# A weights ring 32 bytes lower: the addresses of two operands of TensorE, on a decoder trunk

## The chip, the core and the metric

The kernel runs on one core of a Trainium2 chip. The metric is the device time of one execution in microseconds; the figure for a kernel is the median of its runs. SBUF, the working memory, has 128 partitions; a tile of n float32 columns takes 4n bytes in each, from the same address on. Here "address" always means that byte address within a partition, and "remainder" the address modulo 256.

## The reference, cut to what matters

Two layers of a decoder trunk on x of 512 tokens by 1024 features, all in float32:

```
h  = RMSNorm(x);  p = h @ W_in                      # columns for four mixers and their gates
x += W_o( sum over mixers m of sigmoid(gate_m) * (mixer_m(p) @ P_m) )   # MLA, HGRN2, S5, RWKV-7
x += CrossAttn(RMSNorm(x), RMSNorm(mem))            # 4 heads, 256 memory tokens
x += ConvGLU-FFN(RMSNorm(x))                        # width 2816
```

and a last RMSNorm. Most of the arithmetic is products of an activation matrix with a weight matrix of 1024, 512 or 2816 rows.

## The kernel before

Activations are kept transposed, a tile of 128 features by 512 tokens at a time. Every weight matrix is cut into blocks of 128 x 128, and the host lays all blocks down in the order in which they are used (w_order). `Ring` streams them: eight blocks are a chunk, one DMA fills `raw` (three buffers of 4 KB per partition), ScalarE rounds it into `whi` (line 238) and VectorE makes the rest, `wlo` (line 239; two buffers of each). MLA and the gated unit of S5 have small rings of their own. An activation is split the same way: hh and hl (for the projection, the output, the queries and the feed-forward's first products), oh and ol (mixers' outputs in the merge), ah and al (the feed-forward's last product), mh and ml (memory).

A dense product is then three matmuls per block, into one PSUM bank (`dense`, lines 331 to 333):

```
nc.tensor.matmul(ps[:, :N], hi, xh, start=i == 0, stop=False)
nc.tensor.matmul(ps[:, :N], hi, xl, start=False, stop=False)
nc.tensor.matmul(ps[:, :N], lo, xh, start=False, stop=i == n - 1)
```

The first operand is the stationary one, 128 columns that TensorE loads ahead (LDWEIGHTS in the profile, "PEld"); the second is the moving one, 512 columns (256 for the memory's keys). While a matmul streams its moving operand from one address, the next one's weights are loaded from another. In `dense_t` (lines 353 to 355) the activation is the stationary operand and the ring the moving one.

A layer goes: projection with the four mixers (MLA, HGRN2, S5, RWKV-7) woven into it, their small F32 matmuls between the dense ones; merge with the gates (lines 569 to 587); keys and values of the memory, output projection, cross attention; feed-forward. The order is that of the program, found by a scheduler with priorities; it plays no part in the change.

Where a tile lies is decided by pools. On the left of SBUF they follow each other upwards: `const`, `hp` (hh and hl), `sm` (small statistics), the ring, and then the pools of a stage (memory, x, RWKV-7, MLA, keys and values of the cross attention). On the right other pools grow downwards: HGRN2, S5, merge (oh, ol), queries and probabilities of the cross attention, feed-forward (ah, al). Four tiles named pad0 to pad3 are never read or written; they only take room. In the built program of before, hh, hl, the ring, mh, ml, x, oh, ol, ah, al, q, pT and the keys and values all start at remainder 128; MLA's ring and activations at 160; S5's ring and activations at 128. hh starts at 28288, whi at 74112, wlo at 82304.

The functions that the diff touches follow; lines are those of the profile.

Of the kernel before, what the change touches and what calls it, by code (L numbers as in the profile page):

```python
# [9 lines left out]
F32 = mybir.dt.float32  # L10
# [12 lines left out]
P = 128  # L23
# [189 lines left out]
class Ring:  # L213


    def __init__(self, T, name, pool, raw_bufs, bufs):
        self.T, self.name, self.pool, self.rb, self.b = T, name, pool, raw_bufs, bufs
        self.n = CHUNK[name]
        self.order, self.dram, self.pos = ORDERS[name], T.A[name], 0
        self.raws = {}  # L220
# [32 lines left out]
class Trunk:  # L253
    def __init__(self, ctx, tc, A):
        self.tc, self.nc, self.A, self.ctx = tc, tc.nc, A, ctx
        nc = self.nc
        self.const = self.pool(ctx, "const")
        self.const.tile([P, 48], F32, name="pad0")
        self.hp = self.pool(ctx, "hp")
        self.sm = self.pool(ctx, "sm")  # L260
        self.sm.tile([P, 56], F32, name="pad1")
        self.pool(ctx, "pr", side="right").tile([P, 24], F32, name="pad2")
        self.ps = self.pool(ctx, "ps", space=PSUM)
        self.ring = Ring(self, "w", self.pool(ctx, "ring"), 3, 2)
        self.vec = self.const.tile([P, L, NVEC], F32, name="vec")
        nc.sync.dma_start(out=self.vec, in_=A["vec"])
        self.halves = self.const.tile([P, L, 24], F32, name="halves")
        o = VOFF["w0"]
        nc.vector.tensor_scalar(out=self.halves, in0=self.vec[:, :, o:o + 24], scalar1=0.5, scalar2=None, op0=ALU.mult)
        self.ident = self.const.tile([P, P], F32, name="ident")  # L270
        self.ones = self.const.tile([P, 1], F32, name="ones")
        nc.vector.memset(self.ones, 1.0)
        dp = self.pool(ctx, "dram", space=bass.MemoryType.DRAM)
        self.r_d = [dp.tile([3, 4, P, S], F32, name=f"r_d{l}") for l in range(L)]
        self.xk_d = [dp.tile([KD, P, MEM], F32, name=f"xk_d{l}") for l in range(L)]
        self.c_d = dp.tile([3, P, S], F32, name="c_d")
        self.su_d = dp.tile([4, P, 4, P], F32, name="su_d")
        self.sy_d = dp.tile([4, P, 4, P], F32, name="sy_d")
        self.x_d = dp.tile([KD, P, S], F32, name="x_d")
        self.o_d = [dp.tile([4, P, S], F32, name=f"o_d{m}") for m in range(4)]  # L280
        self.g_d = dp.tile([4, 8, P, S], F32, name="g_d")
# [1356 lines left out]
```

## Time and profile before

| | us |
|---|---|
| median of 3 runs | 2774.59 |
| lowest and highest | 2773.11, 2781.51 |
| profiled execution, its own time | 2776.61 |
| its span, first to last instruction | 2774.5 |

In that span TensorE is busy for 98%, its weight loads for 80%, VectorE for 65%, ScalarE for 40% and GpSimd for 2%; the 16 DMA engines move 114 GB/s on the mean. Matmuls are pipelined: a record of 0.39 us begins before the one ahead of it has ended, so what a stream of them costs is the step from one start to the next, and it is read from a timeline or from a window that holds nothing else. The granted clock stands in the view by windows as a share of full speed. "Idle before" is the time in which an engine had nothing under way, and what ended it.

### The profile page before, as it was taken

Reading aid. Unit: us, or ns where it says so; the run is one execution under the profiler, and the core shown is the slowest. Engines: PE = TensorE matmul, PEld = TensorE weight load, DVE = VectorE, ACT = ScalarE, POOL = GpSimd, SP = SyncE. Lnnn points to the kernel's source line nnn. Section 1 sums busy time; section 2 is a strip of 40 time slices with the busy share of each in tenths; the row PEclk is TensorE's granted clock in tenths of the full one; section 3 lists DMA queues with packets and bytes.
Section 4 is the critical chain, followed back from the end, with each engine's and each line's share of the span. In section 5 each row is a group of like instructions: output and inputs, shape, how many; then the busy total and the mean of one; then the engine's idle time right before and its main releaser. Section 6 shows DMA issues by size and latency. Waiting matters only on the chain.

```text
span 2774.5 us, 37768 instructions
## 1 busy us (share of the span) xinstructions
PE 2714.2 (98%) x14176; PEld 2211.9 (80%) x14176; DVE 1816.6 (65%) x3784; ACT 1112.5 (40%) x1766; POOL 46.5 (2%) x155
## 2 busy tenths in 40 slices
PE   7999999999999999999999999999999999999997
PEld 6878877877788888888888878778777888888886
DVE  6678789675576566546466787797655855664563
ACT  5333343345554443223243333443565534432232
POOL 1000000000000000000000000000000000000000
PEclk9999999999999999999999999999999999999999
DMA  6322233233673233333343232333437632233332
GB/s 196 96 74 71 72 104 103 95 126 110 224 247 120 84 99 97 95 97 99 125 134 99 74 94 63 108 100 98 131 112 254 211 106 77 92 99 98 92 99 76
DMA packets 134534, 315.71 MB, mean 114 GB/s; under 512 B 18384, under 2 KB 38480, under 8 KB 134352
## 3 DMA queue, kind: packets, MB, share of 16 engines
q1 hardware_dynamic: 134352, 313.31, 36.2%
q8 instruction: 112, 1.84, 0.3%
q14 instruction: 70, 0.57, 0.1%
HBM read 266.32 MB, written 45.61 MB: 112 GB/s over the span
## 4 chain that ended last, share of the span: by engine, by line
PE 64%; DVE 5%; DMA 1%; issue 1%; ACT 1%; SPq 0%; DVEq 0%; POOL 0%; ACTq 0%
PE mm L332 17%; PE mm L331 17%; PE mm L333 17%; DVE wlo L239 1%; PE rwy L659 1%; PE hg L1372 1%; PE rw L659 1%; PE mm L354 1%; PE mm L355 1%; PE rw L1520 1%; PE mm L353 1%; PE rw L1016 1%; DVE rdg L924 1%; DVE rdg L926 0%; PE rw L1035 0%
## 5 line engine op out<-in xcount | busy, mean ns | idle before, releaser
L331 PE MATMUL mm<-hh,whi 128*128 128x512 f32 x2144 | 851.2, 397 | 3.1 <-ACT wa L473 2.4
L332 PE MATMUL mm<-hl,whi 128*128 128x512 f32 x2144 | 851.0, 397 | 0.1
L333 PE MATMUL mm<-hh,wlo 128*128 128x512 f32 x2144 | 849.5, 397 | 0.0
L238 ACT ACTIVATE whi<-raw 128x1024 fp32r<-128x1024 f32 (+1 forms) x404 | 418.6, 1037 | 740.5 <-PE mm L332 607.8
L239 DVE TENSOR_TENSOR wlo<-raw,whi 128x1024 fp32r<-128x1024 f32 (+1 forms) x404 | 482.8, 1195 | 294.8 <-ACT whi L238 285.6
L331 PEld LDWEIGHTS mm<-hh,whi 128*128 128x128 f32 x2144 | 404.9, 189 | 88.8 <-ACT wa L473 2.9
L332 PEld LDWEIGHTS mm<-hl,whi 128*128 128x128 f32 x2144 | 405.1, 189 | 85.8 <-issue 4.7
L333 PEld LDWEIGHTS mm<-hh,wlo 128*128 128x128 f32 x2144 | 405.4, 189 | 82.3 <-issue 2.3
L331 PE MATMUL mm<-ah,whi 128*128 128x512 f32 x352 | 136.9, 389 | 0.0
L332 PE MATMUL mm<-al,whi 128*128 128x512 f32 x352 | 136.9, 389 | 0.0
L333 PE MATMUL mm<-ah,wlo 128*128 128x512 f32 x352 | 136.9, 389 | 0.0
L588 DVE TENSOR_TENSOR x<-mm,x 128x512 f32<-128x512 f32 x64 | 44.2, 690 | 123.1 <-PE mm L333 123.1
L331 PE MATMUL mm<-oh,whi 128*128 128x512 f32 x256 | 99.9, 390 | 1.6 <-ACT g L559 1.1
L333 PE MATMUL mm<-oh,wlo 128*128 128x512 f32 x256 | 99.6, 389 | 0.0
L332 PE MATMUL mm<-ol,whi 128*128 128x512 f32 x256 | 99.6, 389 | 0.0
L711 DVE TENSOR_TENSOR gt<-mm,rstd 128x512 f32<-128x512 f32 x44 | 30.5, 692 | 98.2 <-PE mm L333 94.3
L924 DVE TENSOR_TENSOR rdg<-rdg,rE 128x2 f32<-128x2 f32 (+30 forms) x248 | 84.0, 339 | 3.5
L718 ACT ACTIVATE cv<-cv 128x512 f32<-128x512 f32 x44 | 27.8, 632 | 129.7 <-DVE cv L716 129.7
L333 PEld LDWEIGHTS mm<-ah,wlo 128*128 128x128 f32 x352 | 66.1, 188 | 13.7
L331 PEld LDWEIGHTS mm<-ah,whi 128*128 128x128 f32 x352 | 66.1, 188 | 13.7
L332 PEld LDWEIGHTS mm<-al,whi 128*128 128x128 f32 x352 | 66.1, 188 | 13.7
L721 DVE TENSOR_TENSOR up<-mm,rstd 128x512 f32<-128x512 f32 x44 | 30.4, 692 | 63.9 <-PE mm L333 63.9
(511 smaller groups left out, 4158.0 us busy)
## 6 DMA issues: line engine op xcount, KB each, us to landing
raw<-w SPq DMA_DIRECT2D x384, 512.0 KB, 3.6
g_d<-g SPq DMA_DIRECT2D x64, 256.0 KB, 2.1
gin<-g_d SPq DMA_DIRECT2D x64, 256.0 KB, 3.7
oin<-o_d SPq DMA_DIRECT2D x32, 256.0 KB, 3.6
mt<-memT SPq DMA_DIRECT2D x32, 128.0 KB, 3.4
x<-xT SPq DMA_DIRECT2D x16, 256.0 KB, 5.6
raw<-wm SPq DMA_DIRECT2D x12, 256.0 KB, 2.9
xk_d<-xkt SPq DMA_DIRECT2D x16, 128.0 KB, 2.5
```

What stands on the lines that cost most here:

```text
L238: nc.scalar.activation(out=self.hi, in_=raw, func=AF.Copy)
L239: nc.vector.tensor_tensor(out=self.lo, in0=raw, in1=self.hi.bitcast(F32), op=ALU.subtract)
L331: nc.tensor.matmul(ps[:, :N], hi, xh, start=i == 0, stop=False)
L332: nc.tensor.matmul(ps[:, :N], hi, xl, start=False, stop=False)
L333: nc.tensor.matmul(ps[:, :N], lo, xh, start=False, stop=i == n - 1)
L353: nc.tensor.matmul(o, xh[:, ts], wh, start=first, stop=False)
L588: self.nc.vector.tensor_tensor(out=self.x[n], in0=ps, in1=self.x[n], op=ALU.add)
L659: nc.tensor.matmul(out, x, y, start=first and n == 0, stop=last and n == 2)
L711: nc.vector.tensor_tensor(out=gt[:, 2:], in0=ps, in1=rs, op=ALU.mult)
L718: nc.scalar.activation(out=cv, in_=cv, func=AF.Silu)
L721: nc.vector.tensor_tensor(out=up, in0=ps, in1=rs, op=ALU.mult)
L924: V.tensor_tensor(out=tmp[:, :n, :t + 1], in0=M[:, :t + 1, :n].rearrange("p s c -> p c s"), in1=E[:, t, :t + 1].unsqueeze(1).to_broadcast( ...
```

## The change

One pad becomes 32 bytes shorter, 48 float32 columns in place of 56:

```diff
         self.sm = self.pool(ctx, "sm")
-        self.sm.tile([P, 56], F32, name="pad1")
+        self.sm.tile([P, 48], F32, name="pad1")
         self.pool(ctx, "pr", side="right").tile([P, 24], F32, name="pad2")
         self.ps = self.pool(ctx, "ps", space=PSUM)
         self.ring = Ring(self, "w", self.pool(ctx, "ring"), 3, 2)
```

All that is allocated on the left after it starts 32 bytes lower: the small statistics of `sm`, the ring (whi from 74112 to 74080), mh and ml, x, the tiles of RWKV-7, MLA with its ring, and the cross attention's keys and values. `const`, hh and hl lie ahead of it and stay; all on the right stays, with oh, ol, ah, al, q, pT and all of HGRN2 and S5. So ring and hh, hl, ah, al, oh, ol differ by 32 in the remainder instead of 0; ring and mh, ml, and everything within MLA or S5, by 0 as before. The instructions of each engine, their order and their waits are the same in both programs.

## Rows read from the trace of the kernel before

**Rows 1.** Page, part 1: busy time, share of the span and instructions by engine.
```profile
PE 2714.2 (98%) x14176; PEld 2211.9 (80%) x14176; DVE 1816.6 (65%) x3784; ACT 1112.5 (40%) x1766; POOL 46.5 (2%) x155
```

**Rows 2.** View by tile, whi: records in ns (min/median/max), first and last start, shapes.
```profile
L331 PE MATMUL mm<-hh,whi x2144: 387/389/795, 46.4 to 2696.6; 128*128 128x512 f32 x195
...
L238 ACT ACTIVATE whi<-raw x404: 613/1061/1072, 5.3 to 2746.2; 128x1024 fp32r<-128x1024 f32 x126, 128x512 fp32r<-128x512 f32 x9
...
L239 DVE TENSOR_TENSOR wlo<-raw,whi x404: 665/1224/1234, 6.4 to 2747.3; 128x1024 fp32r<-128x1024 f32 x126, 128x512 fp32r<-128x512 f32 x9
...
L331 PE MATMUL mm<-ah,whi x352: 389/389/389, 1148.0 to 2756.4; 128*128 128x512 f32 x176
...
L331 PE MATMUL mm<-oh,whi x256: 389/389/499, 754.2 to 2212.7; 128*128 128x512 f32 x128
```

**Rows 3.** View by windows, tile mm on TensorE: length, busy, count, clock, DMA share.
```profile
1000.00:1388.00 388.00, 386.26 (x1706) 1.00 0.34 102
2370.00:2755.00 385.00, 383.25 (x1690) 1.00 0.30 92
```

**Rows 4.** Timeline of TensorE, 1143 to 1147 us: start, length, line, operation (17 rows).
```profile
1143.24 0.39 PE L331 MATMUL mm<-hh,whi 128*128 128x512 f32 x1
...
1146.86 0.39 PE L332 MATMUL mm<-hl,whi 128*128 128x512 f32 x1
```

**Rows 5.** Timeline of TensorE, 1391 to 1395 us, 256 columns (25 rows).
```profile
1391.78 0.28 PE L331 MATMUL mm<-mh,whi 128*128 128x256 f32 x1
...
1394.66 0.28 PE L331 MATMUL mm<-mh,whi 128*128 128x256 f32 x1
```

**Rows 6.** Timeline of TensorE, 805 to 808 us, layer 0's merge.
```profile
805.29 0.47 PE L331 MATMUL mm<-oh,whi 128*128 128x512 f32 x1 [0.49 <-DVE gin L580]
805.60 0.39 PE L332 MATMUL mm<-ol,whi 128*128 128x512 f32 x1
...
806.75 0.40 PE L331 MATMUL mm<-oh,whi 128*128 128x512 f32 x1
...
807.68 0.39 PE L332 MATMUL mm<-ol,whi 128*128 128x512 f32 x1
```

**Rows 7.** View by lines at 806.76 us: busy, mean ns of one.
```profile
L331 PE MATMUL mm<-oh,whi 128*128 128x512 f32 x1 | 0.4, 397 | 0.0
```

**Rows 8.** Timeline of TensorE, 593 to 595 us: from MLA back to the projection.
```profile
593.12 0.39 PE L332 MATMUL rw<-cql,whi 128*128 128x512 f32 x1
593.35 0.40 PE L333 MATMUL rw<-cqh,wlo 128*128 128x512 f32 x1
...
594.51 0.39 PE L333 MATMUL mm<-hh,wlo 128*128 128x512 f32 x1
```

**Rows 9.** Timeline of the weight loads, near 806.75 and near 1146.86 us.
```profile
806.75 0.19 PEld L332 LDWEIGHTS mm<-ol,whi 128*128 128x128 f32 x1
...
1146.87 0.19 PEld L333 LDWEIGHTS mm<-hh,wlo 128*128 128x128 f32 x1
```

**Rows 10.** By windows, line 332 on TensorE: mixers and merges, both layers.
```profile
90.00:680.00 590.00, 175.84 (x434) 0.99 0.30 94
680.00:940.00 260.00, 135.78 (x349) 1.00 0.57 181
1500.00:2078.00 578.00, 169.00 (x414) 0.99 0.31 95
2078.00:2310.00 232.00, 122.54 (x313) 0.99 0.57 182
```

**Rows 11.** View by lines, shapes apart: out<-moving,stationary; busy us, mean ns.
```profile
L353 PE MATMUL mm<-whi,hh 128*128 128x256 f32 x128 | 38.4, 300 | 0.0
...
L659 PE MATMUL rwy<-pT,xv 128*128 128x512 f32 x96 | 29.5, 412 | 0.0
...
L659 PE MATMUL rw<-xk,q 128*128 128x256 f32 x192 | 28.0, 289 | 0.0
```

**Rows 12.** Page, part 6: DMA issues, KB each, us to landing.
```profile
raw<-w SPq DMA_DIRECT2D x384, 512.0 KB, 3.6
```

## The prediction

> **What bounds the kernel now.** I read the totals by engine first. TensorE is busy for 2714.2 of 2774.5 us and VectorE for 1816.6 [rows 1], so a step pays only through TensorE, and everything added to TensorE's stream counts nearly in full. In the long dense stretches the granted clock is 1.00 [rows 3], its upper level (2.4 GHz), and the change gives it no reason to move.
>
> Then the view by tile of whi: it gives the shortest, median and longest record of each kind of matmul [rows 2]. The 352 records with ah on line 331 all last 389 ns, those with oh and hh have 389 ns as their median. Records overlap, so a record is longer than the step from one start to the next. The step comes from windows and timelines. Two stretches that hold little but the output projection, the queries, the cross attention's output and the feed-forward give 1706 matmuls in 386.26 us and 1690 in 383.25 us [rows 3], 226.4 and 226.8 ns each; I use **226.6 ns**. One piece of the timeline shows it directly: from 1143.24 to 1146.86 us lie 16 steps, 226 ns each [rows 4]. I call that the regular beat.
>
> The beat is not all column time. With 256 columns 24 steps take 2.88 us [rows 5], 120 ns each. The second 256 columns thus cost 106.6 ns, and 120 - 106.6 leaves about **13.4 ns per matmul** that no column explains.
>
> The timeline after a pause is what decides my forecast. At 805.29 us a matmul has waited 0.49 us; from 805.60 to 807.68 nothing waits, yet nine steps take 2.08 us, 231.1 ns each, with records of up to 0.40 us, and only from 807.68 on is it 0.39 and the regular beat [rows 6]. The same instructions on the same tiles run at two paces, and settle in the faster one. In the lines view of that spell one record takes 397 ns [rows 7], 8 more than on the beat. So there is a timing relation between the two reads of TensorE, the moving operand and the next weights, that costs 0 to 8 ns when it is off, and which the present placement lets settle.
>
> One place shows the two reads with different address remainders already. As the built program places them, MLA's weights and activations both start at 160 modulo 256; hh, hl and the main ring at 128. Around 593.35 us the stream changes from one set to the other, so one moving tile is read beside weights 32 bytes away. The record ahead of it is 0.39 and its own 0.40, and five steps from there take 1.16 us, 232 ns each, with no wait named [rows 8]. A single crossing throws the stream off its beat.
>
> **The change part by part.** The pad is one tile; no instruction, wait or DMA is added, removed or reordered on any engine. What moves is the address of everything allocated on the left after it: the rings, the memory tiles mh and ml, x, xk and xv go from 128 to 96 modulo 256. hh, hl, ah, al, oh, ol, q and pT stay.
>
> *Dense matmuls of the main ring.* Each weight block serves three instructions, on lines 331, 332 and 333, as often as one another. With hh and hl that makes 2144 x 3, with ah and al 352 x 3, with oh and ol 256 x 3: 8256 [rows 2]. Those on the beat can lose it; those already off it, behind an interruption, have nothing to lose. The two long stretches hold 1706 + 1690 [rows 3]. The merges with their surroundings hold (349 + 313) x 3 = 1986, with means of 135.78 / 349 = 389 and 122.54 / 313 = 391 ns [rows 10]: close to the beat. The mixers hold (434 + 414) x 3 = 2544 with means of 405 and 408 ns [rows 10], many of them next to a wait or an F32 matmul; with a median of 389 [rows 2] I take half, 1272. Together 1706 + 1690 + 1986 + 1272 = **6654**.
>
> The price of one is not in the trace, since no long stretch has the new difference. From the dear side the 397 ns record gives +8 ns. From the cheap side the whole 13.4 ns could go. Nearest are the two stretches that are off the beat with no wait: 231.1 - 226.6 = 4.5 [rows 6] and 232 - 226.6 = 5.4 [rows 8]. I take **5 ns**: 6654 x 5 = 33.3 us. The weight load starts with the matmul ahead of it to within 0.01 us, on the beat (1146.86 us) and off it (806.75 us) [rows 4, 6, 9], so I see nothing that lets the hardware shift the load by the time of 32 bytes and settle as before.
>
> The Trainium skill, in "TensorE: Matmul & The Clock Gate", section "Step-by-step: what each phase is for", says that TensorE reads moving operand and weights through two independent ports and that loading the next weights takes no read bandwidth from the running matmul. By that rule the sum would be 0 us and not 33. The spells of rows 6 and 8 don't decide against it outright, for they might be a matter of issue; it is the second rival below.
>
> *Smaller products.* In HGRN2's values hh and hl are the weights and the ring the moving operand: 128 x 3 of 256 columns. Queries by keys: 192 of 256. Values by probabilities: 96 of 512 [rows 11]. 672 x 5 ns = 3.4 us; about half stand beside a wait, so 1.7 us.
>
> *What does not change its relation.* Keys and values of the memory (mh, ml and ring move together), MLA (all left) and the gated unit of S5 (all right): 0 us. They are a control inside the kernel.
>
> *VectorE, ScalarE, DMA.* The splits of a chunk take 1061 and 1224 ns by the median [rows 2], while a chunk's 24 matmuls take 24 x 226.6 = 5.4 us; a raw chunk lands after 3.6 us [rows 12] with three buffers. Should the 32 bytes slow any of them by half, they stay hidden; if the landing grew beyond two chunks, 10.9 us, TensorE would wait next.
>
> Sum: 33.3 + 1.7 = **35 us**. The profiled execution took 2776.6 us and would go to 2811.6; it lies 2.0 us above the median of 2774.6 us. From the median: **2810 us**, slower by 1.3%. Likeliest case's own range: 3 to 8 ns, 6654 x 3 = 20 to 6654 x 8 = 53 us, so 2795 to 2830 with the smaller products.
>
> **The rivals.**
>
> *Faster: the fixed 13.4 ns are the price of equal remainders.* If moving operand and weights get in each other's way because they start at the same remainder, 32 bytes would part them. All of it gone: 6654 x 13.4 = 89 us, 2686 us; the case decides from 1.3 ns per matmul on (8.3 us, 0.3%, which is about what a measurement of this kernel can tell from no change). For it: the 13.4 ns are there on the beat in each matmul [rows 4, 5]. Against it: the crossing in MLA, where the difference is 32 already, shows a longer record and not a shorter one [rows 8]. The Trainium skill's page named above gives columns / 2.4 + 2.5 ns as the gap of a warm matmul (section "Back-to-back issue gap"), 216 ns here, which would leave about 11 ns to gain; no stretch read here runs at that. Chance 0.13.
>
> *No change: the addresses don't matter, or the stream settles on an equal beat.* Then the off-beat spells are a matter of issue after a wait, and the crossing in MLA is one of ring or PSUM bank. For it: hh lies an odd and ah an even multiple of 256 bytes from the ring, and both run at 389 ns [rows 2]; the spell with oh has equal remainders throughout [rows 6]. Against it: at the crossing nothing waits. 2775 us. Chance 0.21.
>
> *Dearer: every affected matmul runs at the worst record,* 397 ns, also those that are off the beat now: 8256 x 8 = 66 us and 672 x 8 = 5 us, 2846 us. For it: nothing but that record [rows 7]; a fixed difference could hold the stream at one bad point as well as at a mean. It is the end of the slower case, with 0.08 of its chance.
>
> That the change doesn't do what it says is excluded: in the built program the ring starts 32 bytes lower, and hh, ah and oh stay.
>
> **How the numbers follow.** Slower 0.66 (the forecast with 0.58 and the dearest end with 0.08), no change 0.21, faster 0.13. The range takes in no change with its scatter (2771) and the dearest end (2846); left out are the faster case and a little at both ends, under 2 in 10.
>
> **What would show it.** Right: the records with ah, 389 ns in each of 352 now, go to 392 to 397; the 1706 matmuls of the first long stretch take about 395 us; the 256-column steps with mh stay at 120 ns, since there both operands moved; VectorE, ScalarE and DMA keep their durations. Wrong: ah still at 389 (no change) or well below (faster); or the memory's matmuls slow down as well, which would mean that the distance is not what counts; or more idle time of TensorE behind whi, wlo or raw.

## The result, and the profile after

| | before | after |
|---|---|---|
| median (runs) | 2773.85 us (4) | 2812.98 us (4) |
| lowest and highest | 2772.92, 2781.51 | 2803.09, 2815.53 |
| profiled execution, its own time | 2776.61 | 2813.34 |
| its span | 2774.5 | 2811.1 |

The kernel became slower: the ratio is 1.0126 with an interval of [1.0106, 1.0146], 39 us by the medians and 36.6 us by the two spans. The forecast was 2810 us.

The first line of the page's part 1 answers to [rows 1].

```profile
PE 2756.9 (98%) x14176; PEld 2209.7 (79%) x14176; DVE 1817.7 (65%) x3784; ACT 1113.5 (40%) x1766; POOL 46.5 (2%) x155
```

The same number of instructions on each engine. TensorE's busy time went from 2714.2 to 2756.9 us, 42.7 more; VectorE and ScalarE were busy for 1 us more each, too little for any stage to notice. Span less busy time, the time in which TensorE had nothing under way, went the other way: from 60.3 (2774.5 - 2714.2) to 54.2 us (2811.1 - 2756.9).

The view by tile of whi answers to [rows 2]: records in ns as min/median/max, first and last start.

```profile
L331 PE MATMUL mm<-hh,whi x2144: 387/396/795, 41.7 to 2731.5; 128*128 128x512 f32 x195
...
L331 PE MATMUL mm<-ah,whi x352: 393/395/397, 1161.5 to 2793.1; 128*128 128x512 f32 x176
...
L331 PE MATMUL mm<-oh,whi x256: 392/396/438, 761.3 to 2236.1; 128*128 128x512 f32 x128
...
L331 PE MATMUL mm<-mh,whi x128: 278/283/582, 6.5 to 1433.0; 128*128 128x256 f32 x128
```

Before, every one of the 352 records with ah lasted 389 ns; now the shortest of them lasts 393. The medians of hh and oh went the same way, to 396. The last line is the control inside the kernel: mh moved together with the ring, and its median is 283 ns in both programs. Its line of before is this one.

```profile
L331 PE MATMUL mm<-mh,whi x128: 277/283/582, 6.8 to 1412.4; 128*128 128x256 f32 x128
```

ScalarE's rounding into whi is where it was, at a median of 1060 ns (1061 before).

The view by windows of tile mm on TensorE answers to [rows 3], over nearly the same two stretches of work, which lie 10 to 35 us later.

```profile
1010.00:1405.00 395.00, 393.53 (x1686) 1.00 0.32 99
2400.00:2790.00 390.00, 388.54 (x1664) 1.00 0.29 89
```

393.53 / 1686 = 233.4 ns and 388.54 / 1664 = 233.5 ns a matmul, against 226.4 and 226.8. The clock is 1.00 in both. A piece of the timeline answers to [rows 4]: start and length in us.

```profile
1154.78 0.39 PE L332 MATMUL mm<-hl,whi 128*128 128x512 f32 x1
...
1157.82 0.40 PE L333 MATMUL mm<-hh,wlo 128*128 128x512 f32 x1
```

13 steps in 3.04 us are 233.8 ns each, with no wait, and the records alternate between 0.39 and 0.40. The stream is not ragged: by the starts in the trace its steps repeat as 231, 235, 233, 234 ns. Before they repeated as 227, 227, 226.

To see how many matmuls paid, I took the steps between neighbouring starts in the two traces. TensorE's 14176 matmuls come in the same order in both, so each step can be set against itself. Of the 8256 dense products whose two operands changed their relation, 7671 have a step between 220 and 260 ns in both traces, that is, no interruption in either. 6613 of them were on the beat before (under 229 ns): they went from 226.7 to 233.3 ns on the mean. The other 1058 were off it: 232.9 before, 232.7 after. All 7671 together took 43.9 us more. The unaffected 512-column products (memory, MLA, S5) have as many steps under 229 ns as before, 202 and then 211 of 367, with a mean of 226.6 ns both times.

The smaller products are seen in the view by lines, shapes apart (busy us, mean ns), which answers to [rows 11].

```profile
L353 PE MATMUL mm<-whi,hh 128*128 128x256 f32 x128 | 37.7, 295 | 0.0
...
L659 PE MATMUL rwy<-pT,xv 128*128 128x512 f32 x96 | 29.7, 414 | 0.0
```

The 512-column one became longer by 2 ns a record (412 before). The two with 256 columns became shorter: the one shown from 300 to 295 ns, queries by keys from 289 to 288.

### The profile page after: what moved, and what is told of

It reads as the page before. It is cut to its first block, busy times and chain, and to the rows that moved or that the text cites. A ratio compares the mean times of both kernels' runs of the same rounds, so it can differ in the third digit from the quotient of the medians.

```text
span 2811.1 us, 37768 instructions
## 1 busy us (share of the span) xinstructions
PE 2756.9 (98%) x14176; PEld 2209.7 (79%) x14176; DVE 1817.7 (65%) x3784; ACT 1113.5 (40%) x1766; POOL 46.5 (2%) x155
## 4 chain that ended last, share of the span: by engine, by line
PE 86%; DVE 9%; DMA 2%; ACT 1%; issue 1%; SPq 0%; DVEq 0%; POOL 0%; ACTq 0%; POOLq 0%
PE mm L331 21%; PE mm L332 21%; PE mm L333 21%; DVE wlo L239 2%; PE hg L1372 2%; PE rw L1016 1%; PE rw L1520 1%; DVE rdg L924 1%; DVE rdg L926 1%; PE mm L355 1%; PE mm L353 1%; PE mm L354 1%; PE rwy L659 1%; PE rw L659 1%; PE rw L1035 1%
## 5 line engine op out<-in xcount | busy, mean ns | idle before, releaser
L331 PE MATMUL mm<-hh,whi 128*128 128x512 f32 x2144 | 863.2, 403 | 3.1 <-ACT wa L473 2.4
L332 PE MATMUL mm<-hl,whi 128*128 128x512 f32 x2144 | 862.6, 403 | 0.0
L333 PE MATMUL mm<-hh,wlo 128*128 128x512 f32 x2144 | 861.9, 402 | 0.0
```

## The experiments

Two theories stood at the start. By the **difference theory** a 512-column matmul costs more whenever its moving operand and the weights beside it start at different remainders, wherever they lie. By the **place theory** it is the ring's own new place (96 in place of 128) that costs, whatever the other operand does. Four kernels, all shifts by 32 bytes with the pads, tell them apart; the kernel before had a median of 2776.24 us beside them (21 runs).

**1. hh and hl go down with the ring.** A smaller pad0 in place of pad1 moves hh, hl and all behind them; the right side stays.

```diff
-        self.const.tile([P, 48], F32, name="pad0")
+        self.const.tile([P, 40], F32, name="pad0")
```

> pad0 is 8 columns shorter in place of pad1: hh and hl go down by 32 bytes together with the ring, ah, al, oh, ol stay. Difference theory (the remainder of the moving operand against that of the ring decides): hh and hl are back at difference 0 and on the beat, 226.7 ns; only ah, al (1056 matmuls) and oh, ol (768) pay 233.3 - 226.7 = 6.6 ns as in the changed kernel, 1824 x 6.6 = 12 us: about 2786 us, ah records 393 to 397, hh median 389. Place theory (the ring's own address decides, by traffic of DMA, ScalarE or VectorE around it, not the difference): the ring lies as in the changed kernel, so about 2813 us and hh median 396.

Measured: 2785.26 us (2779.36 to 2788.0), ratio 1.0026 [1.0009, 1.0042]. View by tile of whi:

```profile
L331 PE MATMUL mm<-hh,whi x2144: 387/389/795, 46.0 to 2704.0; 128*128 128x512 f32 x195
...
L331 PE MATMUL mm<-ah,whi x352: 393/396/399, 1147.3 to 2765.6; 128*128 128x512 f32 x176
...
L331 PE MATMUL mm<-oh,whi x256: 393/396/497, 753.3 to 2218.6; 128*128 128x512 f32 x128
```

The ring lies where it lies in the changed kernel, and the matmuls with hh are back at 389 ns. Those with ah and oh, which still differ, last 396. The place theory falls here.

**2. The right side goes down with the ring.** Now ah, al, oh, ol agree with the ring, and hh, hl alone differ.

```diff
-        self.sm.tile([P, 56], F32, name="pad1")
-        self.pool(ctx, "pr", side="right").tile([P, 24], F32, name="pad2")
+        self.sm.tile([P, 48], F32, name="pad1")
+        self.pool(ctx, "pr", side="right").tile([P, 32], F32, name="pad2")
```

> The change, and pad2 8 columns longer, so that ah, al, oh, ol and all else on the right go down by 32 bytes too; hh and hl alone stay behind. Difference theory: ah, al, oh, ol are back at 389 ns; hh and hl (6432 matmuls, some 4800 of them on the beat before) pay 6.6 ns: 4800 x 6.6 = 32 us less some waiting that shrinks, about 2800 to 2806 us, hh median 396. Place theory: 2813 us and ah at 395.

Measured: 2797.64 us (2793.01 to 2809.68), ratio 1.0079 [1.0052, 1.0106]. View by tile of whi:

```profile
L331 PE MATMUL mm<-hh,whi x2144: 388/396/795, 46.1 to 2716.4; 128*128 128x512 f32 x195
...
L331 PE MATMUL mm<-ah,whi x352: 389/389/402, 1154.8 to 2776.3; 128*128 128x512 f32 x176
```

The mirror image of the first. The two ratios together give 0.26% + 0.79% = 1.05%, the whole change 1.26%; the intervals overlap. The steps add up more closely: the uninterrupted steps of the affected dense products, each against itself in the trace of before, take 12.2 us more in the first run and 32.2 in this one, 44.3 together (unrounded), against 43.9 in the whole change.

**3. Everything lower by 32.** pad0 of 40 and pad2 of 32 move the ring, hh, hl and the right side together.

```diff
-        self.const.tile([P, 48], F32, name="pad0")
+        self.const.tile([P, 40], F32, name="pad0")
...
-        self.pool(ctx, "pr", side="right").tile([P, 24], F32, name="pad2")
+        self.pool(ctx, "pr", side="right").tile([P, 32], F32, name="pad2")
```

> pad0 8 columns shorter and pad2 8 longer: everything on the left from hh on and everything on the right 32 bytes lower, all differences among them as before. Difference theory: 2774 us within 0.3%, ah at 389 in every record, hh median 389. Place theory: about 2813 us, since the ring's addresses are those of the changed kernel.

Measured: 2775.4 us (2767.37 to 2785.92), ratio 0.9997 [0.9978, 1.0015]. View by tile of whi:

```profile
L331 PE MATMUL mm<-ah,whi x352: 388/389/390, 1147.1 to 2752.6; 128*128 128x512 f32 x176
```

The ring, hh, hl and the right side start 32 bytes lower than before, and the whole loss is gone. So the common place doesn't count here, only differences do.

**4. The ring 32 bytes higher.** Does the sign matter?

```diff
-        self.sm.tile([P, 56], F32, name="pad1")
+        self.sm.tile([P, 64], F32, name="pad1")
```

> pad1 8 columns longer: the ring and all behind it on the left go up by 32 bytes, so the difference has the other sign. If only the size of the difference counts: about 2813 us, ah at 393 to 397, steps of 233 ns. If the sign counts (in the changed kernel the 256-column products of hi, whose moving operand is the ring and whose weights are hh, took steps of 116.7 ns in place of 119.9): the dense matmuls would take some 3 ns less than on the beat, 223 to 224 ns, and the time would be about 2774 - 6650 x 3 = 2754 us. Place theory: no forecast; anything between.

Measured: 2809.77 us (2806.04 to 2814.67), ratio 1.0117 [1.0086, 1.0148]; ah at 395/396/397. It costs what 32 lower costs. That the other direction might gain something was a wrong guess.

**5, 6, 7, 8. Other distances.** With the difference theory standing, the question was how the price grows with the distance, whether it returns before 256, and whether a distance beats 0. pad1 alone was changed: 40, 24, 8 and 32 columns put the ring 64, 128, 192 and 96 bytes lower than before.

```diff
-        self.sm.tile([P, 56], F32, name="pad1")
+        self.sm.tile([P, 40], F32, name="pad1")
```

> pad1 16 columns shorter: the ring's remainder differs by 64. If any difference spoils the beat alike, 2800 to 2813 us, ah records around 395. If the price grows with the distance, twice that of 32 bytes: 13 ns a matmul, ah at 402, about 2850 us. If the period were 64 bytes, 2775 us and ah at 389.

> pad1 32 columns shorter: the difference is 128. If what counts is the address modulo 256: ah off 389, the time above 2790 us, by as much as is not known. If the period is 128 or less: 2775 us, ah at 389 in every record.

> pad1 48 columns shorter: the difference is 192, which modulo 256 is 64 to the other side. If sign doesn't matter (as 32 lower, 2813, and 32 higher, 2810, suggest): the same as with 64, within 0.3%. If the period is 128: the same as with 64 as well, so only together with the run at 128 does it say something; if the period is 64, 2775 us.

> pad1 24 columns shorter: the difference is 96. The steps so far were 233.4 ns for 32 lower, 32 higher and 192 lower, 232.5 for 128 and 229.0 for 64: always above the 226.8 of equal remainders. If equal remainders are the only beat as fast as that: 229 to 233.5 ns and 2785 to 2813 us. If other differences can be as good or better: 2775 us or less.

**9. 16 bytes.** Pads move a tile by whole units of 32 bytes here; so whi and wlo were made 64 columns longer and the weights put 4 columns into them. All lines after it are one higher.

```diff
-            self.hi = self.pool.tile([P, w], F32R, tag="whi", name="whi", bufs=self.b)
-            self.lo = self.pool.tile([P, w], F32R, tag="wlo", name="wlo", bufs=self.b)
+            o, e = (4, 64) if self.name == "w" else (0, 0)
+            self.hi = self.pool.tile([P, w + e], F32R, tag="whi", name="whi", bufs=self.b)[:, o:o + w]
+            self.lo = self.pool.tile([P, w + e], F32R, tag="wlo", name="wlo", bufs=self.b)[:, o:o + w]
```

> whi and wlo of the main ring lie 16 bytes into tiles that are 256 bytes longer: the difference is 16. If every difference but 0 modulo 256 costs: steps near 233 ns and about 2809 us. If only whole 32 bytes count: 2775 us and ah at 389. In between, with 16 bytes half as far off: about 2790 us.

The scan, put together. "Step" is the mean step in the longest unbroken series of dense matmuls, by the starts in the trace (1542 or 1543 steps, a few longer ones at its head among them); "in 250 us" is the count of mm matmuls from 2450 to 2700 us in the view by windows.

| ring against hh | median us | ratio, interval | step, ns | in 250 us |
|---|---|---|---|---|
| 0 (before) | 2773.85 to 2776.24 | 1 | 226.8 | 1104 |
| 0, all lower | 2775.40 | 0.9997 [0.9978, 1.0015] | 226.8 | 1104 |
| +16 | 2806.08 | 1.0108 [1.0085, 1.0132] | 233.4 | 1074 |
| +32 | 2809.77 | 1.0117 [1.0086, 1.0148] | 233.4 | 1073 |
| -32 (after) | 2812.98 | 1.0126 [1.0106, 1.0146] | 233.4 | 1074 |
| -64 | 2785.09 | 1.0044 [1.0026, 1.0063] | 229.0 | 1094 |
| -96 | 2810.80 | 1.0126 [1.0099, 1.0152] | 233.4 | 1073 |
| -128 | 2808.96 | 1.0119 [1.0096, 1.0142] | 232.5 | 1078 |
| -192 | 2808.34 | 1.0122 [1.0098, 1.0145] | 233.4 | 1073 |

The rows of the windows view for 0 and for 64 lower are these.

```profile
2450.00:2700.00 250.00, 250.00 (x1104) 1.00 0.32 97
```

```profile
2450.00:2700.00 250.00, 250.00 (x1094) 1.00 0.32 97
```

The price does not grow with the distance. 16 bytes cost as much as 32, 96 or 192; at 128 the steps are less regular (228 to 241 ns) with nearly the same mean. Only 64 lower is cheap, with steps of 226, 229, 232. I had expected 192 lower, which is 64 in the other direction, to do as 64, and it pays in full: so the price there depends on the sign, or on something that 64 lower happens to fit, and it has no period of 128. No distance beats 0.

The scatter between runs of one kernel goes with the granted clock: of the 21 runs of before beside the first four experiments, the shortest (2766.88 us) had a mean of 0.994 and the longest (2788.47 us) 0.986. The steps are taken in a stretch at 1.00 and are free of it.

**10. Only one meeting in three differs.** wlo alone was shifted by 32 bytes, with two pads around it in the ring's pool (32 + 224 bytes, so that what lies behind the two buffers of wlo is back at the old remainder). All lines after them are four higher: 335 is 331. whi meets its neighbours at equal remainders; wlo meets hh and hl at a difference.

```diff
+            if self.name == "w" and not c:
+                self.pool.tile([P, 8], F32, name="pad4")
             self.lo = self.pool.tile([P, w], F32R, tag="wlo", name="wlo", bufs=self.b)
+            if self.name == "w" and not c:
+                self.pool.tile([P, 56], F32, name="pad5")
```

> Two pads in the ring, so that wlo alone lies 32 bytes off and all else is as before (lines from 240 on are higher by 4, 331 to 333 are 335 to 337). Next-weights theory (the moving operand of a matmul against the weights that are loaded during it): only the matmul ahead of a wlo block, hl on line 336, meets a difference. Own-weights theory: only the matmul with wlo on line 337. If each meeting pays for itself, a third of the 6650 pays 6.6 ns: +15 us, 2790 us, and records tell which third (395 to 397 on line 336 or on 337, 389 on the others). If one meeting in three throws the whole stream off its beat, as rows 8 suggest: records of 393 to 397 on all three lines and 2805 to 2813 us.

Measured: 2808.97 us (2806.78 to 2817.66), ratio 1.0132 [1.011, 1.0154], as dear as the whole change. The timeline of TensorE shows how one odd meeting spreads:

```profile
1100.03 0.40 PE L335 MATMUL mm<-hh,whi 128*128 128x512 f32 x1
1100.27 0.40 PE L336 MATMUL mm<-hl,whi 128*128 128x512 f32 x1
1100.51 0.39 PE L337 MATMUL mm<-hh,wlo 128*128 128x512 f32 x1
1100.73 0.40 PE L335 MATMUL mm<-hh,whi 128*128 128x512 f32 x1
```

The steps are 0.24, 0.24 and 0.22 us in every triple; by the starts 233, 239 and 228 ns, 233.4 on the mean. One step of three is nearly on the old beat, another pays double. So the price is not one of each matmul by itself: it belongs to the stream as a whole. The forecast that the records of all three lines go to 393 to 397 failed. In the views by tile those with ah and whi on line 335 all last 395 ns, and the other two lines are these:

```profile
L336 PE MATMUL mm<-al,whi x352: 400/400/400, 1159.1 to 2790.4; 128*128 128x512 f32 x176
...
L337 PE MATMUL mm<-ah,wlo x352: 389/389/397, 1159.3 to 2790.7; 128*128 128x512 f32 x176
```

The longest is the matmul ahead of the one with wlo, with which the load of wlo starts. The one that uses wlo keeps 389 ns, though its moving operand and its own weights are the pair that differs; so if that pair counts, the price shows in other matmuls than its own.

**11. Equal remainders of the moving operand and the next weights.** The weight load of a matmul starts with the matmul ahead of it [rows 9], so while one streams, the weights read beside it are taken to be the next one's. If that pair is all that counts, the beat must come back when each moving tile agrees with the weights loaded during it, though it differs from its own. Shifting wlo by 32, and hl, al and ol by 32 as well, does that: hh streams while whi is loaded (both at the old remainder), hl while wlo is (both 32 higher).

```diff
+                self.pool.tile([P, 8], F32, name="pad4")
...
+                self.pool.tile([P, 56], F32, name="pad5")
...
-        self.sm.tile([P, 56], F32, name="pad1")
+        self.sm.tile([P, 48], F32, name="pad1")
...
+            self.hp.tile([P, 8], F32, name="pad6")
...
+                    pool.tile([P, 8], F32, name="pad7")
...
+                    pool.tile([P, 56], F32, name="pad8")
...
+                    pool.tile([P, 8], F32, name="pad9")
...
+                    pool.tile([P, 56], F32, name="pad10")
```

> Pads put wlo, hl, al and ol 32 bytes off whi, hh, ah and oh. A block's three matmuls then read, as moving operand against the weights loaded during it: xh against whi of the same block, xl against wlo, xh against the next block's whi, all at difference 0; each against its own weights: 0, 32, 32. Next-weights theory: the beat of 226.7 ns stays (ah and al at 389 on all three lines) and the time is 2775 us, although no less differs than in the run with wlo alone (2809). Own-weights theory, or one by which any step of 32 bytes from one operand to the next spoils the beat: 2800 to 2813 us, records of 393 to 400. The 256-column products with mh, ml and in hi are not kept equal; they move the time by 1 to 2 us at most.

Measured: 2806.05 us (2796.51 to 2811.16), ratio 1.0105 [1.0074, 1.0136]. View by tile of whi:

```profile
L335 PE MATMUL mm<-hh,whi x2144: 387/396/795, 44.3 to 2729.7; 128*128 128x512 f32 x195
...
L335 PE MATMUL mm<-ah,whi x352: 392/396/398, 1163.9 to 2791.0; 128*128 128x512 f32 x176
```

The beat does not come back; the steps wander between 226 and 236 ns, 232.3 on the mean. That this pair alone decides is refuted. In this kernel the moving tile also differs from its own weights in two of three matmuls, and moving tiles and weights differ from the ones ahead of them. Nor is it certain which matmul a load lies beside: records of 389 ns at steps of 227 overlap, so the matmul before the one ahead may still be reading when the load starts, and that pair differs in two of three cases here. Which of these counts stays open: no run here shifts one of them without another.

Beside the runs with the ring 64, 128 and 192 lower and with wlo alone shifted, the kernel before had a median of 2775.23 us (13 runs); beside 96 lower, 16 bytes and the last one 2775.15 us (7 runs).

## Why the prediction was right, and where its terms were off

**That TensorE bounds the kernel and the rest hides** held: busy time of VectorE, ScalarE and GpSimd within 1.1 us of [rows 1], a raw chunk still lands after 3.6 us, and the clock of the long stretches stayed at 1.00.

**That the beat depends on the difference of remainders** held and is shown by the runs: the same matmuls pay or don't as the difference is made or undone (experiments 1 to 3). The crossing in MLA [rows 8] pointed the right way, on thin ground: by the starts, the two steps ahead of it take 227 ns and its own 235, but the five ahead of those were off the beat as well (228 to 236), with equal remainders.

**The price of one was too low.** I put 5 ns from two short spells; the settled stream pays 6.7 (226.66 to 233.32 ns over the 6613 steps). Two decimals aren't the reason: by the starts the spells have 231.2 and 232.2 ns. They were too few steps on the way from one pace to another, with some as short as 225 and 228 ns among them; all the uninterrupted steps of 229 ns and more in the trace of before, 1058 of them, have a mean of 232.9, which would have given 6.2.

**The count was good**: 6654 forecast on the beat, 6613 found step by step. The half taken for the mixers was an assumption; this agreement bears it out only in the sum. The products off the beat before pay nothing (232.9 to 232.7), which is what the forecast assumed of them.

**The smaller products had the wrong sign.** I added 1.7 us for them. The 256-column products with hh as weights became faster: by 300 uninterrupted steps, each against itself, from 119.4 to 118.3 ns, which is 0.3 us; with the interrupted ones all 384 took 1.0 us less. (The 119.9 and 116.7 ns in the expectation of the fourth run are too far apart: they are near the commonest steps, 120 and 117, and not the means.)

**The waits were not counted.** I let TensorE's idle time stand; it shrank by 60.3 - 54.2 = 6.1 us. Step against step, the 36.7 us by which the span grew (36.6 by the rounded spans) fall into parts. The uninterrupted steps of the affected products took 43.9 us more. Steps in or within 1 us of a drop of the granted clock in either trace, and those of the first 14 us, took 2.0 more; all others 8.9 less, and the first matmul came 0.3 earlier. In the four other kernels with a dear stream whose lines agree with those of before (32 higher; 96, 128, 192 lower) that third part is 7.5 to 10.9 us, with everything lower it is 2.4. That work of the other engines has longer to be ready when the stream is slower is the natural reading, but it isn't shown wait by wait.

The second part is luck, and a sum of larger ones of both signs, because the clock drops at other times in each execution. These rows of the windows view (TensorE; the clock is the third figure from the right) are before and after:

```profile
0.00:50.00 50.00, 37.36 (x223) 0.90 0.73 236
...
0.00:50.00 50.00, 38.25 (x243) 1.00 0.76 247
```

So the first matmul with hh started at 41.7 us in place of 46.4 [rows 2], which is no work of the addresses: with the ring 192 lower it started at 46.2. From 264 to 302 us the kernel after had 0.78 where before had 1.00, and lost some 7 us again.

Put together: 43.9 + 2.0 - 8.9 - 0.3 = 36.7. The forecast's 33.3 + 1.7 = 35 came out near because a price that was a quarter too small stood against some 9 us of shorter waits and other steps that were left out. The agreement to 2 us with the spans is better than its terms deserve.

**The rivals.** "Faster" (the fixed 13.4 ns is the price of equal remainders) is refuted for 512 columns: seven other differences were tried, none is below 226.8 ns. "No change" is refuted; its best argument, that hh lies an odd and ah an even multiple of 256 from the ring and both run at 389 ns, was true and only says that the remainder modulo 256 is what counts. The Trainium skill ("TensorE: Matmul & The Clock Gate", section "Step-by-step: what each phase is for") says that moving operand and weights have ports of their own and that the load takes no bandwidth from the matmul. By that rule the change would have left 2774 us. The trace disagrees as far as the time goes: same instructions, a clock of 1.00 in both, 233.4 ns in place of 226.8. The measurement decides; whether the ports themselves are what is shared, no run here shows. The dearest end, 8 ns for all, did not come: no distance is above 233.4.

**The marks that were named** came: ah at 393 to 397; mh's and ml's 256-column products unchanged, at a median record of 283 ns for mh and steps of 119.8 and 119.7 ns (300 uninterrupted ones of both, step against step); the first long stretch's 1706 matmuls at 233.4 ns would take 398 us, where I wrote about 395.

## What to carry to other kernels

Where a stream of TensorE has a new weight load for each matmul and is the bound, read the steps between starts in a steady stretch, not the records: a few ns in each came to a per cent of this kernel, and no wait shows them. For matmuls of 512 columns in F32R, as here, let the moving operands and both halves of the weights start at the same remainder modulo 256 bytes, and look at the built addresses again after any edit that adds or shortens a tile ahead of them, since a 32-byte tile shifts everything behind it. Where a pace can be read only from short spells beside an interruption, gather all such steps of the trace before a price is put on them, and give it a range that reaches past them. Where two kernels run the same instructions in the same order, set each step against itself before totals are compared: here it parts the change from what the clock did.

## What the runs showed of the hardware that was not expected

- The price is nearly a step and not a slope: 16 bytes cost 6.7 ns of 226.7, as do 32, 96 and 192; 128 costs 5.7 and 64 lower 2.2.
- One odd meeting in three makes the stream as dear as three odd ones (233.4 ns both), by a repeating 233, 239, 228. From 2450 to 2700 us the mean step is 226.67 ns before and 233.33 to 233.34 after and with 16 bytes, 32 higher, 96 and 192 lower and wlo alone, though each of them repeats other steps. At the upper clock level, 2.4 GHz, which was granted there, that makes 544 and 560 cycles: an estimate worked out from these steps.
- The same differences speed up 256-column products a little. In HGRN2's values the uninterrupted steps have 119.4 ns before, 119.1 and 119.3 where hh and ring agree again (experiments 1 and 3), 118.3 after, 118.2 in experiment 2, and 116.0 with the ring 64 lower.
- With 512 columns, no difference tried took away any of the 13.4 ns that no column explains. The Trainium skill's page named above gives columns / 2.4 + 2.5 ns as the gap of a single, isolated warm matmul (section "Back-to-back issue gap"). No steady stretch read here runs at the 216 ns which that makes for 512 columns; the shortest means are near 226.7.
